# A Poisson loss kernel: loads of two rows per partition, three buffers per input, and a tapered last group

## The chip, the cores and the metric

The kernel runs on one core of one Trainium2 chip. The metric is device time in microseconds (us); a profile taken of one of the executions adds the span from its first to its last instruction, which is some 2 us shorter. All runs reported here are of the fast state, with a granted clock of 1.0. "Unit" below means 128 columns, 512 bytes in each partition. SBUF and PSUM are the two on-chip memories in which the kernels place their tiles, here 128 partitions each. "The same", "faster" and "slower" are meant by a rule of 2%, with a 95% interval for the ratio.

## The reference

```python
# log_input, target: float32 [1024, 4096]
def reference(log_input, target):
    loss = np.exp(log_input) - target * log_input
    return np.mean(loss, axis=-1).astype(np.float32)
```

Two inputs of 16.8 MB each are read once, 1024 numbers are written. ScalarE (ACT) does the exp with its row sum, VectorE (DVE) the product with its row sum.

## The kernel before

Partition p holds rows 8p to 8p+7, so a load of one "row block" takes one row of 16 KB for each of 128 partitions. Four buffers per input; the last row block is cut into pieces of 2048, 1024, 512 and 512 columns.

```python
x_blk = log_input.rearrange("(p b) d -> b p d", b=nb)      # nb = 8
last_bounds = [0, 2048, 3072, 3584, 4096]
io_pool = ctx.enter_context(tc.tile_pool(name="io", bufs=4))
for b in range(nb):
    # ... bounds = [0, d], or last_bounds for the last block
    for c in range(ncy):
        # ... x_tile, t_tile from io_pool
        nc.sync.dma_start(out=x_tile[:, :w], in_=x_blk[b, :, lo:hi])
        nc.sync.dma_start(out=t_tile[:, :w], in_=t_blk[b, :, lo:hi])
        # ACT: exp of x into a bf16 scratch in SBUF, row sum into exp_sums
        # DVE: -t * x into a bf16 scratch, row sum into prod_sums
    # DVE: comb = sum(exp_sums + prod_sums) / d  -> all_loss[:, b]
nc.sync.dma_start(out=out_blk, in_=all_loss)
```

Of the kernel before, what the change touches and what calls it, by code (L numbers as in the profile page):

```python
# [2 lines left out]

# [4 lines left out]


@with_exitstack
def kernel(
    ctx: ExitStack,
    tc: tile.TileContext,
    log_input: bass.AP,
    target: bass.AP,
    out: bass.AP,
):
    nc = tc.nc
    P = nc.NUM_PARTITIONS  # L20
    fp32 = mybir.dt.float32
    bf16 = mybir.dt.bfloat16

    n, d = log_input.shape
    assert target.shape == (n, d)
    assert out.shape == (n,)

    nb = (n + P - 1) // P
    assert nb * P == n, "row count must be a multiple of 128"
    inv_d = 1.0 / d  # L30

    x_blk = log_input.rearrange("(p b) d -> b p d", b=nb)
    t_blk = target.rearrange("(p b) d -> b p d", b=nb)
    out_blk = out.rearrange("(p b) -> p b", b=nb)

    full_bounds = [0, d]
    if d == 4096:
        last_bounds = [0, 2048, 3072, 3584, 4096]
    else:
        last_bounds = [0]  # L40
        rem = d
        while rem > max(512, d // 8):
            rem //= 2
            last_bounds.append(d - rem)
        last_bounds.append(d)
        last_bounds = sorted(set(last_bounds))
    max_chunks = max(len(full_bounds), len(last_bounds)) - 1

    io_pool = ctx.enter_context(tc.tile_pool(name="io", bufs=4))
    accum_pool = ctx.enter_context(tc.tile_pool(name="accum", bufs=4))  # L50
    out_pool = ctx.enter_context(tc.tile_pool(name="outp", bufs=1))
    scratch_pool = ctx.enter_context(tc.tile_pool(name="scratch", bufs=2))

    all_loss = out_pool.tile([P, nb], fp32)

    for b in range(nb):
        bounds = last_bounds if b == nb - 1 else full_bounds
        ncy = len(bounds) - 1

        exp_sums = accum_pool.tile([P, max_chunks], fp32, name="exp_sums")  # L60
        prod_sums = accum_pool.tile([P, max_chunks], fp32, name="prod_sums")

        for c in range(ncy):
            lo, hi = bounds[c], bounds[c + 1]
            w = hi - lo
            x_tile = io_pool.tile([P, d], fp32, name="x_tile")
            t_tile = io_pool.tile([P, d], fp32, name="t_tile")
            nc.sync.dma_start(out=x_tile[:, :w], in_=x_blk[b, :, lo:hi])  # L68
            nc.sync.dma_start(out=t_tile[:, :w], in_=t_blk[b, :, lo:hi])  # L69

            e_scr = scratch_pool.tile([P, d], bf16, name="e_scr")
            nc.scalar.activation(  # L72
                out=e_scr[:, :w],
                in_=x_tile[:, :w],
                func=mybir.ActivationFunctionType.Exp,
                bias=0.0,
                scale=1.0,
                accum_out=exp_sums[:, c:c + 1],
            )

            p_scr = scratch_pool.tile([P, d], bf16, name="p_scr")
            nc.vector.tensor_tensor_reduce(  # L82
                out=p_scr[:, :w],
                in0=t_tile[:, :w],
                in1=x_tile[:, :w],
                scale=-1.0,
                scalar=0.0,
                op0=mybir.AluOpType.mult,
                op1=mybir.AluOpType.add,
                accum_out=prod_sums[:, c:c + 1],  # L90
            )

        comb = accum_pool.tile([P, max_chunks], fp32, name="comb")
        nc.vector.tensor_tensor_reduce(  # L94
            out=comb[:, :ncy],
            in0=exp_sums[:, :ncy],
            in1=prod_sums[:, :ncy],
            scale=inv_d,
            scalar=0.0,
            op0=mybir.AluOpType.add,  # L100
            op1=mybir.AluOpType.add,
            accum_out=all_loss[:, b:b + 1],
        )

    nc.sync.dma_start(out=out_blk, in_=all_loss)


# [1 line left out]
_INS = ['log_input', 'target']  # L109
_OUTS = [((1024,), 'float32')]  # L110


# [23 lines left out]
```

## Time and profile before

| | before |
|---|---|
| device time, median | 87.24 us (87.16 to 87.39, 3 runs) |
| span of the profile | 85.2 us |
| bytes read | 33.55 MB, 394 GB/s over the span |
| first data packet / last load landed / store issued | 1.73 / 81.67 / 82.88 us |

The page's groups of instructions say where the engines wait (columns: line, engine, operation, tiles, shapes and count; then busy us and mean ns of one; then the idle time ahead of the group and what ended it):

```profile
L82 DVE CUSTOM_DVE_ANT_0 p_scr<-t_tile,x_tile 128x4096 bf16<-128x4096 f32 (+3 forms) x11 | 35.9, 3261 | 44.4 <-DMA t_tile<-in_target_dram 44.2
L72 ACT ACTIVATE e_scr<-x_tile 128x4096 bf16<-128x4096 f32 (+3 forms) x11 | 29.5, 2685 | 49.3 <-DMA x_tile<-in_log_input_dram 43.2
```

DVE works 36 us and waits 44 us for t; ACT works 30 us and waits for x. Both wait for the stream.

Beside its views, the trace holds a record of each DMA packet (start, duration, bytes) on the 16 DMA engines, and the text uses those: one packet is one contiguous run of one partition, one descriptor (the 14 loads of 16 KB rows are 1792 packets of 16,384 bytes, 128 each). That makes 8 packets per engine for a load of one row block, and after them each engine makes a 4-byte completion write (352 for 22 loads). "Last completions" below is the mean over the 16 engines of the start of their last completion write of the loads, counted from the first data packet.

### The profile page before, as it was taken

To read this page: it belongs to the slowest core of one execution; us is meant where nothing else is said; L and a number is where in the kernel's file an instruction comes from. 1 tells how busy PE (TensorE), PEld (TensorE's weight loads), DVE (VectorE), ACT (ScalarE), POOL (GpSimd) and SP (SyncE) were. 2 spreads that over 40 slices of the span, in tenths; PEclk is the share of its full clock that TensorE was granted. 3 is DMA by queue.
4 is the path that set the end of the run, shared out by engine and by line. 5 is a ranking of instruction groups with operands and counts; after the bars stand their busy time and mean duration, and the time that the engine had idled before them with its cause. 6 is when DMAs were issued, how large, how long until landed. Compare 5 with 4: busy or idle time off the path is not lost.

```text
span 85.2 us, 165 instructions
## 1 busy us (share of the span) xinstructions
DVE 37.3 (44%) x38; ACT 31.8 (37%) x23; POOL 0.2 (0%) x4
## 2 busy tenths in 40 slices
DVE  0000009920398007930199005950099103989750
ACT  6002940079000960049200880029400690274430
POOL 0000000000000000000000000000000000000000
DMA  5699999999999999999998989899999999999900
GB/s 123 277 462 400 462 400 462 400 462 400 462 400 462 400 462 400 462 400 462 385 477 369 492 369 485 377 462 400 454 408 431 431 431 396 419 406 401 387 22 2
DMA packets 3312, 33.56 MB, mean 394 GB/s; under 512 B 496, under 2 KB 496, under 8 KB 1264
## 3 DMA queue, kind: packets, MB, share of 16 engines
q1 hardware_dynamic: 3312, 33.56, 93.9%
HBM read 33.55 MB, written 0.00 MB: 394 GB/s over the span
## 4 chain that ended last, share of the span: by engine, by line
DMA 80%; DVE 11%; SPq 3%; issue 1%; DVEq 0%
DMA t_tile<-in_target_dram 80%; DVE p_scr L82 11%; SPq L68 2%; SPq L69 1%; DVE comb L94 0%; DVEq L82 0%; DVE prod_sums L82 0%; DVEq L94 0%; DVEq L131 0%
## 5 line engine op out<-in xcount | busy, mean ns | idle before, releaser
L82 DVE CUSTOM_DVE_ANT_0 p_scr<-t_tile,x_tile 128x4096 bf16<-128x4096 f32 (+3 forms) x11 | 35.9, 3261 | 44.4 <-DMA t_tile<-in_target_dram 44.2
L72 ACT ACTIVATE e_scr<-x_tile 128x4096 bf16<-128x4096 f32 (+3 forms) x11 | 29.5, 2685 | 49.3 <-DMA x_tile<-in_log_input_dram 43.2
L72 ACT ACTIVATION_READ_ACCUMULATOR e_scr<-x_tile 128x1 f32 x11 | 2.0, 186 | 0.0
L94 DVE CUSTOM_DVE_ANT_0 comb<-exp_sums,prod_sums 128x1 f32<-128x1 f32 (+1 forms) x8 | 1.3, 160 | 1.2
L72 ACT ACT_TABLE_LOAD x1 | 1.3, 1283 | 0.7 <-PEq L120 0.7
L82 DVE DVE_READ_ACCUMULATOR2_ANT prod_sums<- 128x1 f32 x11 | 0.9, 82 | 0.0
L94 DVE DVE_READ_ACCUMULATOR2_ANT all_loss<- 128x1 f32 x8 | 0.7, 82 | 0.0
L120 POOL MEMSET const-uint8-127<- 128x1 uint8 x1 | 0.1, 102 | 0.0
L120 POOL MEMSET const-bfloat16-1.0<- 128x1 bf16 x1 | 0.1, 101 | 0.0
L120 POOL MEMSET const-float32-0.0<- 128x1 f32 x1 | 0.1, 98 | 0.2 <-issue 0.2
L120 POOL MEMSET const-float32-1.0<- 128x1 f32 x1 | 0.1, 98 | 0.0
## 6 DMA issues: line engine op xcount, KB each, us to landing
x_tile<-in_log_input_dram SPq DMA_DIRECT2D x7, 2048.0 KB, 29.6
t_tile<-in_target_dram SPq DMA_DIRECT2D x7, 2048.0 KB, 34.1
x_tile<-in_log_input_dram SPq DMA_DIRECT2D x1, 1024.0 KB, 27.2
t_tile<-in_target_dram SPq DMA_DIRECT2D x1, 1024.0 KB, 29.3
x_tile<-in_log_input_dram SPq DMA_DIRECT2D x1, 512.0 KB, 21.2
t_tile<-in_target_dram SPq DMA_DIRECT2D x1, 512.0 KB, 22.1
x_tile<-in_log_input_dram SPq DMA_DIRECT2D x2, 256.0 KB, 9.2
t_tile<-in_target_dram SPq DMA_DIRECT2D x2, 256.0 KB, 9.5
```

The costliest lines, as they stand in the source:

```text
L68: nc.sync.dma_start(out=x_tile[:, :w], in_=x_blk[b, :, lo:hi])
L69: nc.sync.dma_start(out=t_tile[:, :w], in_=t_blk[b, :, lo:hi])
L72: nc.scalar.activation(out=e_scr[:, :w], in_=x_tile[:, :w], func=mybir.ActivationFunctionType.Exp, bias=0.0, scale=1.0, accum_out=exp_sums ...
L82: nc.vector.tensor_tensor_reduce(out=p_scr[:, :w], in0=t_tile[:, :w], in1=x_tile[:, :w], scale=-1.0, scalar=0.0, op0=mybir.AluOpType.mult, ...
L94: nc.vector.tensor_tensor_reduce(out=comb[:, :ncy], in0=exp_sums[:, :ncy], in1=prod_sums[:, :ncy], scale=inv_d, scalar=0.0, op0=mybir.AluO ...
L120: nc = _bacc.Bacc("TRN2", target_bir_lowering=False, num_devices=1)
```

## The change

Its intent: move the same bytes in longer runs and fewer transfers, hold more of them in SBUF, and leave less work behind the last byte. Rows are taken in pairs (32 KB runs); the exp's unused output goes to PSUM and the product over t, in place of scratch tiles in SBUF (four of 8 KB per partition), and each input has three 32 KB buffers; the last group is cut so that x comes ahead of t, and the last product takes all earlier sums as a pointer scalar (one start value per partition, read from SBUF, in place of a constant), so that no combine, the small instruction that adds up a row's sums, follows it.

```diff
-    io_pool = ctx.enter_context(tc.tile_pool(name="io", bufs=4))
+    x_v = log_input.rearrange("(p g r) d -> g p (r d)", g=groups, r=2)
+    tail = [
+        ("x", 32 * u), ("t", 32 * u), ("x", 24 * u), ("t", 12 * u), ("t", 12 * u),
+        ("x", 6 * u), ("t", 5 * u), ("x", 2 * u), ("t", 3 * u),
+    ]
+    io = ctx.enter_context(tc.tile_pool(name="io", bufs=3))
+    dump = ctx.enter_context(tc.tile_pool(name="dump", bufs=1, space=bass.MemoryType.PSUM))
 ...
+    for g in range(groups - 1):
+        x_tile = io.tile([P, 2 * d], F32, name="x_tile")
+        t_tile = io.tile([P, 2 * d], F32, name="t_tile")
+        nc.sync.dma_start(out=x_tile, in_=x_v[g])
+        nc.sync.dma_start(out=t_tile, in_=t_v[g])
 ...  # for each of the two rows: exp_sum, prod_sum (over t), combine
+    for what, w in tail:
 ...
+                combine(slice(nb - 1, k["t"]), so_far)
+                prod_sum(x_tile, t_tile, s, -inv_d, so_far, all_loss[:, b : b + 1])
```

More of the change, by code (lines that the diff above doesn't have):

```diff
@@ L2 @@
-import math
 from contextlib import ExitStack
@@ L8 @@
 from concourse._compat import with_exitstack
+ACT_F = mybir.ActivationFunctionType
+ALU = mybir.AluOpType
+F32 = mybir.dt.float32
 @with_exitstack
@@ L20 @@
     P = nc.NUM_PARTITIONS
-    fp32 = mybir.dt.float32
-    bf16 = mybir.dt.bfloat16
     n, d = log_input.shape
-    assert target.shape == (n, d)
-    assert out.shape == (n,)
-    nb = (n + P - 1) // P
-    assert nb * P == n, "row count must be a multiple of 128"
+    nb = n // P
+    assert nb * P == n and tuple(target.shape) == (n, d) and nb % 2 == 0
+    assert d % 32 == 0
     inv_d = 1.0 / d
-    x_blk = log_input.rearrange("(p b) d -> b p d", b=nb)
-    t_blk = target.rearrange("(p b) d -> b p d", b=nb)
@@ L34 @@
-    out_blk = out.rearrange("(p b) -> p b", b=nb)
-    full_bounds = [0, d]
-    if d == 4096:
-        last_bounds = [0, 2048, 3072, 3584, 4096]
-    else:
-        last_bounds = [0]
-        rem = d
-        while rem > max(512, d // 8):
-            rem //= 2
-            last_bounds.append(d - rem)
-        last_bounds.append(d)
-        last_bounds = sorted(set(last_bounds))
-    max_chunks = max(len(full_bounds), len(last_bounds)) - 1
-    io_pool = ctx.enter_context(tc.tile_pool(name="io", bufs=4))
@@ L50 @@
-    accum_pool = ctx.enter_context(tc.tile_pool(name="accum", bufs=4))
-    out_pool = ctx.enter_context(tc.tile_pool(name="outp", bufs=1))
-    scratch_pool = ctx.enter_context(tc.tile_pool(name="scratch", bufs=2))
-    all_loss = out_pool.tile([P, nb], fp32)
-    for b in range(nb):
-        bounds = last_bounds if b == nb - 1 else full_bounds
-        ncy = len(bounds) - 1
-        exp_sums = accum_pool.tile([P, max_chunks], fp32, name="exp_sums")
-        prod_sums = accum_pool.tile([P, max_chunks], fp32, name="prod_sums")
-        for c in range(ncy):
-            lo, hi = bounds[c], bounds[c + 1]
-            w = hi - lo
-            x_tile = io_pool.tile([P, d], fp32, name="x_tile")
-            t_tile = io_pool.tile([P, d], fp32, name="t_tile")
-            nc.sync.dma_start(out=x_tile[:, :w], in_=x_blk[b, :, lo:hi])
-            nc.sync.dma_start(out=t_tile[:, :w], in_=t_blk[b, :, lo:hi])
-            e_scr = scratch_pool.tile([P, d], bf16, name="e_scr")
-            nc.scalar.activation(
-                out=e_scr[:, :w],
-                in_=x_tile[:, :w],
-                func=mybir.ActivationFunctionType.Exp,
-                bias=0.0,
-                scale=1.0,
-                accum_out=exp_sums[:, c:c + 1],
-            )
-            p_scr = scratch_pool.tile([P, d], bf16, name="p_scr")
-            nc.vector.tensor_tensor_reduce(
-                out=p_scr[:, :w],
-                in0=t_tile[:, :w],
-                in1=x_tile[:, :w],
-                scale=-1.0,
-                scalar=0.0,
-                op0=mybir.AluOpType.mult,
-                op1=mybir.AluOpType.add,
-                accum_out=prod_sums[:, c:c + 1],
-            )
-        comb = accum_pool.tile([P, max_chunks], fp32, name="comb")
-        nc.vector.tensor_tensor_reduce(
-            out=comb[:, :ncy],
-            in0=exp_sums[:, :ncy],
-            in1=prod_sums[:, :ncy],
@@ new lines @@
+    groups = nb // 2
+    u = d // 32
+    x_v = log_input.rearrange("(p g r) d -> g p (r d)", g=groups, r=2)
+    t_v = target.rearrange("(p g r) d -> g p (r d)", g=groups, r=2)
+    out_v = out.rearrange("(p b) -> p b", b=nb)
+    tail = [
[3 more added lines that the diff above has]
+    io = ctx.enter_context(tc.tile_pool(name="io", bufs=3))
+    small = ctx.enter_context(tc.tile_pool(name="small", bufs=1))
@@ new lines, with exp_sum @@
+    dump = ctx.enter_context(tc.tile_pool(name="dump", bufs=1, space=bass.MemoryType.PSUM))
+    exp_sums = small.tile([P, nb + 4], F32, name="exp_sums")
+    prod_sums = small.tile([P, nb + 4], F32, name="prod_sums")
+    comb = small.tile([P, nb], F32, name="comb")
+    so_far = small.tile([P, 1], F32, name="so_far")
+    all_loss = small.tile([P, nb], F32, name="all_loss")
+    def exp_sum(x_tile, s, k):
+        e_scr = dump.tile([P, d], F32, name="e_scr")
+        nc.scalar.activation(
+            out=e_scr[:, : s.stop - s.start],
+            in_=x_tile[:, s],
+            func=ACT_F.Exp,
+            bias=0.0,
+            scale=1.0,
+            accum_out=exp_sums[:, k : k + 1],
+        )
@@ new lines, in prod_sum, with combine @@
+    def prod_sum(x_tile, t_tile, s, scale, start, accum):
+        nc.vector.tensor_tensor_reduce(
+            out=t_tile[:, s],
+            in0=t_tile[:, s],
+            in1=x_tile[:, s],
+            scale=scale,
+            scalar=start,
+            op0=ALU.mult,
+            op1=ALU.add,
+            accum_out=accum,
+        )
+    def combine(k, accum):
+        nc.vector.tensor_tensor_reduce(
+            out=comb[:, : k.stop - k.start],
+            in0=exp_sums[:, k],
+            in1=prod_sums[:, k],
@@ L98 @@
             scale=inv_d,
             scalar=0.0,
-            op0=mybir.AluOpType.add,
-            op1=mybir.AluOpType.add,
-            accum_out=all_loss[:, b:b + 1],
-        )
-    nc.sync.dma_start(out=out_blk, in_=all_loss)
+            op0=ALU.add,
+            op1=ALU.add,
+            accum_out=accum,
+        )
+    for g in range(groups - 1):
[3 more added lines that the diff above has]
+        nc.sync.dma_start(out=t_tile, in_=t_v[g])
+        for r in range(2):
+            b = 2 * g + r
+            s = slice(r * d, (r + 1) * d)
+            exp_sum(x_tile, s, b)
+            prod_sum(x_tile, t_tile, s, -1.0, 0.0, prod_sums[:, b : b + 1])
+            combine(slice(b, b + 1), all_loss[:, b : b + 1])
@@ new lines @@
+    g, b = groups - 1, nb - 1
+    x_tile = io.tile([P, 2 * d], F32, name="x_tile")
+    t_tile = io.tile([P, 2 * d], F32, name="t_tile")
+    at = {"x": 0, "t": 0}
+    k = {"x": nb - 2, "t": nb - 2}
+    for what, w in tail:
+        s = slice(at[what], at[what] + w)
+        at[what] += w
+        if what == "x":
+            nc.sync.dma_start(out=x_tile[:, s], in_=x_v[g, :, s])
+            exp_sum(x_tile, s, k["x"])
+        else:
+            nc.sync.dma_start(out=t_tile[:, s], in_=t_v[g, :, s])
+            if s.stop < 2 * d:
+                prod_sum(x_tile, t_tile, s, -1.0, 0.0, prod_sums[:, k["t"] : k["t"] + 1])
+                if s.stop == d:
+                    combine(slice(nb - 2, nb - 1), all_loss[:, b - 1 : b])
+            else:
+                combine(slice(nb - 1, k["t"]), so_far)
+                prod_sum(x_tile, t_tile, s, -inv_d, so_far, all_loss[:, b : b + 1])
+        k[what] += 1
@@ L109 @@
+    assert at == {"x": 2 * d, "t": 2 * d} and k["x"] == k["t"] - 1 == nb + 2
+    nc.sync.dma_start(out=out_v, in_=all_loss)
 _INS = ['log_input', 'target']
```

## The prediction

> **What bounds the kernel now.** I read the page first: engines, slices, queue, chain. The question it answers is which resource is full from start to end.
>
> ```profile
> DVE 37.3 (44%) x38; ACT 31.8 (37%) x23; POOL 0.2 (0%) x4
> DMA  5699999999999999999998989899999999999900
> DMA packets 3312, 33.56 MB, mean 394 GB/s; under 512 B 496, under 2 KB 496, under 8 KB 1264
> q1 hardware_dynamic: 3312, 33.56, 93.9%
> DMA 80%; DVE 11%; SPq 3%; issue 1%; DVEq 0%
> ```
>
> Neither compute engine is half busy. The DMA row is at 9 from the third slice until the loads are in, and the chain is 80% one kind of wait, a landing of the target tensor. So the kernel is a stream of 33.55 MB with a start before it and a tail behind it, and a change can win only in three places: the rate of the stream, its start, and what follows its last byte.
>
> The stretches of time give the rate (columns: stretch, its length, busy us of DVE, ACT and POOL, clock, DMA share, GB/s):
>
> ```profile
> 12.00:22.00 10.00, 4.60 (x4) 3.71 (x2) 0.00 (x0) 1.00 1.01 434
> 22.00:71.00 49.00, 23.01 (x20) 18.55 (x10) 0.00 (x0) 1.00 1.00 428
> 71.00:76.00 5.00, 4.41 (x2) 1.96 (x2) 0.00 (x0) 1.00 1.00 415
> 76.00:79.00 3.00, 2.49 (x6) 1.20 (x3) 0.00 (x0) 1.00 1.02 402
> 79.00:81.00 2.00, 1.71 (x3) 0.72 (x2) 0.00 (x0) 1.00 1.04 381
> ```
>
> The share stays at 1.00 or above in all five, so the queue never ran dry; yet the rate falls from 428 to 381 GB/s as the pieces of the last row block get smaller. That is a cost for each descriptor. The packet records of the trace give it directly. Median times on an engine: 612 ns for 16 KB, 312 for 8 KB, 162 for 4 KB, 87 for 2 KB, 9 for a 4-byte completion write. The first four lie on one line: 12 ns plus 36.6 ns per KB (16,384 bytes in 600 ns; 16 engines: 437 GB/s).
>
> Last the chain in order of time (start, us, what), for what follows the last landing:
>
> ```profile
> 76.46 5.21 DMA t_tile<-in_target_dram
> 81.67 0.03 issue
> 81.70 0.05 DVEq L82
> 81.75 0.08 issue
> 81.84 0.69 DVE p_scr L82
> 82.53 0.02 DVE prod_sums L82
> ...
> 82.68 0.16 DVE comb L94
> ```
>
> From the landing at 81.67 there are 0.17 us to the start of the last product, 0.69 for it, 0.15 to the combine and 0.16 for that; the store is issued at 82.88, 1.21 us after the landing. The remaining 2.3 us of the span are the store and the end of the program, which the change leaves alone.
>
> [...]
>
> **The change part by part.**
>
> *Rows of 32 KB.* Before, each of 16 engines handles 8 partitions of each load: 14 loads of 16 KB make 112 descriptors, and the eight tail pieces 64 more (16 of 8 KB, 16 of 4 KB, 32 of 2 KB): 176. After, six loads of 32 KB make 48, and nine pieces of the last group 72: 120. The 56 fewer descriptors are worth 56 x 12 = 0.67 us. Loads fall from 22 to 15, so 7 completion writes of 9 ns go: 0.06. Together 0.73 us, all of it on the path, because the engines are never idle. A check of this model on the kernel before: 2,097,152 bytes per engine at 600 ns per 16,384 are 76.8 us, 176 x 12 are 2.1, 22 x 9 are 0.2: 79.1 us. The packet records run from 1.7 to 81.2 us, 79.4, and the first packets took up to 1420 ns instead of 612; that accounts for the rest.
>
> *Three buffers per input.* The last group's loads wait for the first group's buffers. I put the first t landing at about 22 us and its two products at 2 x 4.43 us, so the buffers are free near 31.5. Five more 4 MB loads are then queued or in flight, enough until about 61 us. The builder's order of instructions also shows that each load waits for the completion of the eighth load before it, as its eight completion semaphores come round; with these sizes each such landing is over ten microseconds ahead of need. So no hole: worth 0.
>
> *In-place product, exp into PSUM.* The product writes fp32 over t instead of bf16 elsewhere[...]. Both engines have over 50% idle time in the stream. Worth 0 there.
>
> *The tail.* The last t piece is 384 wide instead of 512[...], and no combine stands behind it; but now a combine (so_far) stands ahead of it, and that needs the exp of the last x piece. I set the last landing to T. A piece of n units (512 bytes per partition) takes 8 x (18.75n + 12) + 9 ns, so the landings are: x of 2 units T-0.56, t of 5 T-0.96, x of 6 T-1.82, second t of 12 T-2.82, first T-4.73. ACT, by 0.203 us plus 0.833 ns per element (fitted to 512: 630 and 4096: 3616): the 768 exp runs from T-1.65 and is out with its accumulator read by T-0.71; the 256 exp starts at T-0.39, takes 0.42, with the read it ends at T+0.12. DVE: the 1536 products (1.76 us each) end at T-2.80 and T-0.89, the 640 one runs from T-0.79 to T+0.04. The combine can start near T+0.2, so_far is there at T+0.38, the last product starts after 0.15 more at T+0.54 and ends at T+1.10, the store goes out at T+1.13. Before it was T+1.21. Gain 0.08, well within the error of these gaps.
>
> *Start.* The first load is issued and its first packet starts as before. Worth 0.
>
> Sum: 0.73 + 0.08 = 0.81 us; 87.24 - 0.81 = 86.43. I round it to 86.45.
>
> **The rivals.**
>
> *The 32 KB rows are cut again.* [...]the count is 168 instead of 120, and the gain is 8 x 12 + 63 = 0.16 us for the stream: about 87.0. Nothing in the trace before has a row over 16 KB, so it speaks neither way; I give it one chance in five.
>
> *A new wait in the tail.* The new order chains exp, accumulator read, combine and product after the last x landing, and puts the 640 product ahead of it. If each hand-over between engines costs 0.1 us more than I took, or a product with a pointer scalar starts later, the store goes out at T+1.4: a loss of 0.2 instead of a gain of 0.08, 86.7. For it speaks that the margin between DVE and ACT is under 0.2 us; against it that each link has a measured duration.
>
> *A hole in the stream.* If the last group's issue were held longer than I think, DMA would idle between groups and the time would rise by some microseconds. Against it: about 30 us of margin. I give it 2%.
>
> *A large gain.* It would need the start or the rate to move. The start is latency ahead of the first packet; with no descriptor cost at all the rate would gain 2.1 us, 2.4%, and the change keeps over two thirds of the descriptors. I give it 2%.
>
> **Range and chances.** The middle is 86.45; the split rows or the longer tail lie to 87.0, both together near 87.25. On the lower side, a shorter tail (PSUM as destination, a smaller gap ahead of the last product) gives at most 0.3. The runs of before spread over 0.23 us. So 86.05 to 87.0 in 8 of 10. Faster by over 2% would be under 85.5: 0.02. Slower by over 2% would be above 89.0: 0.02. The rest, 0.96, is within 2%.
>
> **What would show each step right or wrong.** The queue's packet count: 48 x 16 + 72 x 16 data packets, 128 of the store and 16 x 16 completions are 2304; 3072 would mean split rows. A 32 KB packet of about 1212 ns. First exp near 12.5 us, first product near 22.3, later first products of a group 19.4 us apart (two loads of 8 x 1.212 + 0.009), not 19.57 (twice the 9.785 us between products now). DMA row at 9 until the last landing, which comes near 80.9 instead of 81.67. Store issued about 1.1 us after it. The prediction is wrong if any slice in the middle falls below 9, if the landing stays at 81.5 or later without split rows, or if the store follows the last landing by more than 1.5 us.

The sum came to 0.81 us, 0.73 for the stream and 0.08 for the tail; the working for the last product had 0.56 us for 384 columns, where 512 took 0.69. The tail's product times are estimates, and the trace before gives the same ones: the line through its products of 512 and 4096 columns (692 and 4425 ns) comes to 1.76 us for 1536 columns, 0.83 for 640 and 0.56 for 384; measured later were 1758 and 826 ns, and 559 for 384 in e3. That a product over t takes as long as before was not shown then; for 4096 columns it took 4423 ns against 4425. Cut rows mean 168 packets per engine, two of 16 KB for each 32 KB row; why they should be cut was not shown. The wait for the eighth load before is in the changed kernel's trace: its loads 12 to 15 were issued at 41.90, 51.61, 61.33 and 66.22 us, 0.02 us after loads 4 to 7 had landed. The "at most 0.3" for a shorter tail is the author's estimate without working; what PSUM gave is 29 ns per exp (e6).

## The result, and the profile after

The changed kernel takes 86.69 us (86.65 to 86.79, 4 runs) against 87.31 for the kernel before in the same job (87.16 to 87.40): ratio 0.9934, 95% interval 0.9920 to 0.9948. A ratio here is the mean time of one kernel's fast runs over the mean of the other's fast runs of the same rounds, so it is not quite the ratio of the medians quoted. By the 2% rule this is "same"; the gain of 0.62 us is small but clear of noise. A repeat in another job gave 0.9966.

The page of the changed kernel, the same rows as in the prediction:

```profile
DVE 36.8 (44%) x38; ACT 31.5 (37%) x21; POOL 0.2 (0%) x4
DMA  8597999799979997999799979997999999999900
DMA packets 2304, 33.56 MB, mean 397 GB/s; under 512 B 384, under 2 KB 640, under 8 KB 1152
q1 hardware_dynamic: 2304, 33.56, 93.7%
DMA 92%; SPq 2%; DVE 2%; issue 1%; DVEq 0%
```

The packets are 2304, exactly the count for whole 32 KB rows. The time of all packets is 93.7% of 84.6 us, 79.3 us per engine, against 93.9% of 85.2, 80.0 us: it fell by 0.7 us, about the predicted amount. The stream itself did not end 0.7 us earlier, but about 0.5. DVE's share of the chain fell from 11% to 2% because the chain no longer passes through a product that frees a buffer: it is one run of landings.

The 7s in the DMA row are not idle engines. The view counts a packet whole in the slice in which it starts, which is why slices of 496 GB/s stand beside slices of 325. The 16 engines run nearly in step (their completions of one load lie within 0.42 us) with 1.2 us packets, and slices are 2.1 us long; in a run below with 8 KB packets the same row is 9 all through, with a later end. The completions of the changed kernel's 4 MB loads come 9.681 to 9.712 us apart with no gap.

The stretches of time:

```profile
22.00:71.00 49.00, 27.09 (x24) 18.54 (x10) 0.00 (x0) 1.00 0.99 426
71.00:76.00 5.00, 4.60 (x4) 1.11 (x1) 0.00 (x0) 1.00 0.99 415
76.00:79.00 3.00, 2.15 (x3) 1.74 (x2) 0.00 (x0) 1.00 0.99 400
```

The share is 0.99 where it was 1.00 to 1.02 before, at much the same rate. These last digits alone would prove little, as a packet counts where it starts. The records show what is behind them: in the kernel before, eight packets of 2 KB and a completion write last 8 x 87 + 9 = 705 ns, but the completions of such loads come 676 to 680 ns apart. So the packets of one engine overlap a little in time, here by 4%, while for the 32 KB packets (8 x 1213 + 9 = 9713 ns, steps of up to 9712) the overlap is all but gone.

The end of the chain in order of time, and the row of DMA issues for the last piece:

```profile
80.54 0.83 DVE t_tile L70
81.37 0.02 DVE prod_sums L70
...
81.52 0.14 DVE comb L82
81.65 0.05 DVE so_far L82
81.70 0.04 issue
81.74 0.62 DVE t_tile L70
```

```profile
t_tile<-in_target_dram SPq DMA_DIRECT2D x1, 192.0 KB, 15.0
```

The last t piece was issued at 66.22 us and took 15.0 to land, so the last landing T is at 81.2 (81.23 in the record of landings), 0.44 earlier than before (81.67). The store goes out at 82.39, T+1.16, against T+1.21 before. The last product does not wait for that landing, but for the product and the combine ahead of it.

| | before | after |
|---|---|---|
| packets of data per engine | 176 | 120 |
| last completions (mean of engines) | 79.34 | 78.82 |
| last landing | 81.67 | 81.23 |
| store issued | 82.88 | 82.39 |
| span | 85.2 | 84.6 |

### The profile page after: what moved, and what is told of

Its sections match the earlier page's. It is cut to its first block, busy times and chain, and to the rows that moved or that the text cites. A ratio compares the mean times of both kernels' runs of the same rounds, so it can differ in the third digit from the quotient of the medians.

```text
span 84.6 us, 144 instructions
## 1 busy us (share of the span) xinstructions
DVE 36.8 (44%) x38; ACT 31.5 (37%) x21; POOL 0.2 (0%) x4
## 2 busy tenths in 40 slices
DMA packets 2304, 33.56 MB, mean 397 GB/s; under 512 B 384, under 2 KB 640, under 8 KB 1152
## 3 DMA queue, kind: packets, MB, share of 16 engines
q1 hardware_dynamic: 2304, 33.56, 93.7%
## 4 chain that ended last, share of the span: by engine, by line
DMA 92%; SPq 2%; DVE 2%; issue 1%; DVEq 0%
DMA x_tile<-in_log_input_dram 58%; DMA t_tile<-in_target_dram 34%; DVE t_tile L70 2%; SPq L97 1%; SPq L96 1%; DVE comb L82 0%; DVE so_far L82 0%; DVEq L82 0%; DVEq L70 0%; DVE prod_sums L70 0%; DVEq L154 0%
## 5 line engine op out<-in xcount | busy, mean ns | idle before, releaser
L70 DVE CUSTOM_DVE_ANT_0 t_tile<-t_tile,x_tile 128x4096 f32<-128x4096 f32 (+2 forms) x10 | 35.1, 3530 | 44.7 <-DMA t_tile<-in_target_dram 44.7
L60 ACT ACTIVATE e_scr<-x_tile 128x4096 f32<-128x4096 f32 (+3 forms) x10 | 29.0, 2905 | 49.1 <-DMA x_tile<-in_log_input_dram 49.0
L70 DVE CUSTOM_DVE_ANT_0 t_tile<-t_tile,x_tile,so_far 128x384 f32<-128x384 f32 x1 | 0.6, 619 | 0.1
```

The costliest lines, as they stand in the source:

```text
L60: nc.scalar.activation(out=e_scr[:, : s.stop - s.start], in_=x_tile[:, s], func=ACT_F.Exp, bias=0.0, scale=1.0, accum_out=exp_sums[:, k : ...
L70: nc.vector.tensor_tensor_reduce(out=t_tile[:, s], in0=t_tile[:, s], in1=x_tile[:, s], scale=scale, scalar=start, op0=ALU.mult, op1=ALU.ad ...
```

## The experiments

The main theory: the gain is the 56 descriptors that went, at about 8 ns of elapsed time each, not the 12 ns that the packet durations suggested. Rivals: buffers, scratch or the tail made the gain.

### Rows of 16 KB in the changed kernel (e1)

```diff
-        nc.sync.dma_start(out=x_tile, in_=x_v[g])
-        nc.sync.dma_start(out=t_tile, in_=t_v[g])
+        for r in range(2):
+            h = slice(r * d, (r + 1) * d)
+            nc.sync.dma_start(out=x_tile[:, h], in_=x_v[g, :, h])
+            nc.sync.dma_start(out=t_tile[:, h], in_=t_v[g, :, h])
```

> The changed kernel with its six 32 KB-row loads cut back to twelve of 16 KB rows, all else kept: 48 more descriptors on each DMA engine and 6 more completion writes of 9 ns. Theory A (the gain is descriptors, each worth about 8 ns of elapsed time, as the steps between completions suggest): 48 x 8 + 6 x 9 = 0.44 us more than the changed kernel, about 87.1 us. Theory B (12 ns each, as my prediction had it): 0.63 us more, about 87.3. Rival C (the gain comes from buffers, scratch or the tail, and row length is worth nothing): no change, 86.7.

86.99 us median (86.94 to 88.05) against 87.20 for the kernel before; ratio 0.9997 (0.9963 to 1.0030), widened by the one run at 88.05. By the medians two thirds of the gain are gone (0.21 us left of 0.62). Last completions: 79.28, 0.47 later than the changed kernel's 78.82. Taking off six completions of 9 ns, 48 descriptors cost 0.41 us: 8.6 ns each. By these completions rival C falls, and 8 ns fits better than 12; the times alone would not settle it, as the interval of this ratio takes in the 0.9966 of the changed kernel's repeat (e9 below).

### The kernel before with 32 KB rows (e2)

```diff
-    io_pool = ctx.enter_context(tc.tile_pool(name="io", bufs=4))
+    io_pool = ctx.enter_context(tc.tile_pool(name="io", bufs=2))
-    scratch_pool = ctx.enter_context(tc.tile_pool(name="scratch", bufs=2))
+    scratch_pool = ctx.enter_context(tc.tile_pool(name="scratch", bufs=1))
 ...
-            x_tile = io_pool.tile([P, d], fp32, name="x_tile")
-            t_tile = io_pool.tile([P, d], fp32, name="t_tile")
-            nc.sync.dma_start(out=x_tile[:, :w], in_=x_blk[b, :, lo:hi])
-            nc.sync.dma_start(out=t_tile[:, :w], in_=t_blk[b, :, lo:hi])
+            if b < nb - 2:
+                if b % 2 == 0:
+                    # ... x_pair, t_pair [P, 2 * d]
+                    nc.sync.dma_start(out=x_pair, in_=x2_blk[b // 2])
+                    nc.sync.dma_start(out=t_pair, in_=t2_blk[b // 2])
+                # ... the half of the pair that holds row b
+            else:
+                # ... rows 6 and 7 in pieces as before, one tile for all pieces of a row
-                out=p_scr[:, :w],
+                out=t_tile[:, :w],
```

> The kernel before with only its first six row blocks loaded as three pairs of 32 KB rows, its tail and its combines kept (the product is written over t to make room). 48 descriptors and 6 completion writes fewer than before. Theory A (8 ns): 0.44 us faster than before, about 86.87. Theory B (12 ns): 0.63 faster, about 86.7. Rival C (row length worth nothing): as before, 87.3.

86.64 us median (86.56 to 87.19) against 87.20; ratio 0.9945 (0.9926 to 0.9963), which is 0.32 to 0.65 us. The interval holds A and just holds B; the packet records speak for A: last completions at 78.96, 0.37 earlier than in the kernel before, or 6.7 ns for each of 48 descriptors. So the long rows give nearly the whole gain in the old kernel, without the PSUM destination, the new pieces and the fold. (Buffers and scratch were changed with them here; e7 shows that two buffers are no gain of their own.)

### The combine after the last product (e3)

```diff
+    nc.vector.memset(exp_sums, 0.0)
-                combine(slice(nb - 1, k["t"]), so_far)
-                prod_sum(x_tile, t_tile, s, -inv_d, so_far, all_loss[:, b : b + 1])
+                prod_sum(x_tile, t_tile, s, -1.0, 0.0, prod_sums[:, k["t"] : k["t"] + 1])
+                combine(slice(nb - 1, k["t"] + 1), all_loss[:, b : b + 1])
```

> The changed kernel with the last product not folded: no pointer scalar, a combine of four columns after it instead of one of three ahead of it. The last product can then start as soon as the product ahead of it is done, about 0.2 us after the last landing instead of 0.51, takes 0.56 instead of 0.62, and 0.32 us of gap and combine follow: store at about T+1.1, against T+1.16 now. Theory: within 0.1 us of the changed kernel (86.6 to 86.7). Rival (the fold is where the tail gains): slower by 0.3 us, 87.0.

86.50 us median (86.35 to 86.62) against 87.20; ratio 0.9921 (0.9908 to 0.9934). Its last completions are the changed kernel's (78.83), and its end in the chain reads:

```profile
81.36 0.56 DVE t_tile L72
81.92 0.02 DVE prod_sums L72
...
82.07 0.17 DVE comb L84
```

The store goes out at 82.27 instead of 82.39, with the last landing at 81.23 in both. In these profiles the fold of the combine into the last product is thus no gain but a loss of about 0.1 us: the combine and the 0.15 us ahead of it stand on DVE either way, the fold adds a second hand-over (0.04 us, from the combine to the product), and the product with a pointer scalar takes 619 ns where the one without takes 559. (The memset clears a column that the combine reads and no exp fills.)

### The old pieces in the changed kernel (e4)

```diff
-        ("x", 32 * u), ("t", 32 * u), ("x", 24 * u), ("t", 12 * u), ("t", 12 * u),
-        ("x", 6 * u), ("t", 5 * u), ("x", 2 * u), ("t", 3 * u),
+        ("x", 32 * u), ("t", 32 * u), ("x", 16 * u), ("t", 16 * u), ("x", 8 * u), ("t", 8 * u),
+        ("x", 4 * u), ("t", 4 * u), ("x", 4 * u), ("t", 4 * u),
```

(The combine stands last here too, as in e3.)

> The changed kernel with the pieces of the kernel before in its last row block (2048, 1024, 512, 512 for each input, x and t by turns, combine last). Eight descriptors and one completion write more (0.07 us by 8 ns) and the store at T+1.21 instead of T+1.16: 0.12 us more than the changed kernel, about 86.8. Rival (the taper is most of the gain): 0.4 to 0.6 more, 87.1 to 87.3.

86.74 us median (86.54 to 87.06) against 87.20; ratio 0.9949 (0.9935 to 0.9963), by that 0.1 us behind the changed kernel. Last completions 78.94. As expected, for the pieces and the fold together. What the pieces alone are worth is seen against e3, which has the same order of combine and ran in the same job; the two stores, e3 and then this run:

```profile
82.27 0.35 SPq L130 DMA_DIRECT2D out_dram<-all_loss  x1
82.48 0.35 SPq L131 DMA_DIRECT2D out_dram<-all_loss  x1
```

The old pieces are 0.21 us later (0.24 by the ratios 0.9949 and 0.9921). So the taper is worth about 0.2 us, half of it in earlier completions (78.83 against 78.94), and the fold took about half of that back.

### A dose of descriptors (e5)

```diff
-        nc.sync.dma_start(out=x_tile, in_=x_v[g])
+        for h in (slice(0, d // 2), slice(d // 2, d)):
+            nc.sync.dma_start(
+                out=x_tile.rearrange("p (r d) -> p r d", r=2)[:, :, h],
+                in_=x_v[g].rearrange("p (r d) -> p r d", r=2)[:, :, h],
+            )
 ...  # t likewise
```

> A dose: the changed kernel with each 4 MB load made as two of half the columns of both rows, so that every run is 8 KB: 192 descriptors of 8 KB per engine in place of 48 of 32 KB, 144 more, and 6 more completion writes. Theory A (8 ns elapsed per descriptor): 144 x 8 + 54 = 1.2 us more than the changed kernel, about 87.9. Theory B (12 ns): 1.8 us more, about 88.5. If row length is worth nothing: 86.7.

88.00 us median (87.90 to 88.11) against 87.31; ratio 1.0072 (1.0050 to 1.0094). Relative to the kernel before it lost 0.69 us by the medians where the changed kernel gained 0.62: 1.3 us apart, and A said 1.2, B 1.8. Last completions 80.22, 1.40 later for 144 descriptors and six completions: 9.4 ns each. This run and e1 have the same 21 loads and differ in 96 descriptors alone; their completions lie 0.93 us apart, 9.7 ns each, so it is not the number of loads that costs. Its page:

```profile
DMA  3899999999999999999999999999999999999900
DMA packets 4704, 33.56 MB, mean 390 GB/s; under 512 B 480, under 2 KB 736, under 8 KB 1248
```

The engines look busier than in the changed kernel, and the kernel is slower.

### Exp to SBUF again (e6)

```diff
-    dump = ctx.enter_context(tc.tile_pool(name="dump", bufs=1, space=bass.MemoryType.PSUM))
+    dump = ctx.enter_context(tc.tile_pool(name="dump", bufs=1))
-        e_scr = dump.tile([P, d], F32, name="e_scr")
+        e_scr = dump.tile([P, d], mybir.dt.bfloat16, name="e_scr")
```

> The changed kernel with the exp written as bf16 to SBUF again instead of fp32 to PSUM. My theory (both engines idle over half the time, the 256-wide exp is not what the combine waits for last): no change within 0.1 us, exp of 4096 back at about 3.62 us. Rival (less traffic on SBUF is part of the stream's gain): 0.1 to 0.3 us slower and later completions in the packet records.

86.60 us median (86.40 to 86.89) against 87.31; ratio 0.9914 (0.9888 to 0.9941). Exp of 4096 took 3616 ns again, against 3587 with PSUM; last completions 78.88 against 78.82. An fp32 result in PSUM in place of a bf16 one in SBUF (place and type changed together) gives the engine 29 ns per exp (388 ns against 417 for 256 columns too) and the kernel nothing.

### Two buffers (e7)

```diff
-    io = ctx.enter_context(tc.tile_pool(name="io", bufs=3))
+    io = ctx.enter_context(tc.tile_pool(name="io", bufs=2))
```

> The changed kernel with two buffers per input instead of three. The third group's loads then wait for the first group's products, free near 31.5 us, while the queue holds loads until about 41 us. Theory: no hole, no change within 0.1 us (86.7). Rival (three buffers are needed to keep the queue full): a hole of microseconds, 88 or more, and a slice of the DMA row well below 9.

86.59 us median (86.37 to 86.86) against 87.31; ratio 0.9915 (0.9889 to 0.9940), last completions 78.84. The third group's loads waited 28.7 us for a product, and the stream did not notice:

```profile
SPq L96 <- DVE prod_sums L70: 28.7, 1, 28.7
```

The third buffer is worth nothing. (This run's DMA row has single slices of 6 and 7, as the changed kernel's has 7s, so that part of the expectation was badly chosen; the completions are 9.681 to 9.718 us apart.)

### Rows of 48 KB (e8): a miss

```diff
-    io = ctx.enter_context(tc.tile_pool(name="io", bufs=3))
+    io = ctx.enter_context(tc.tile_pool(name="io", bufs=2))
-    for g in range(groups - 1):
-        x_tile = io.tile([P, 2 * d], F32, name="x_tile")
+    for g in range(2):
+        x_tile = io.tile([P, 3 * d], F32, name="x_tile")
 ...  # t likewise
+        nc.sync.dma_start(out=x_tile[:, : 3 * d], in_=x_r[:, 3 * g * d : 3 * (g + 1) * d])
-        for r in range(2):
+        for r in range(3):
```

> The change carried one step further: groups of three, three and two rows, so four loads of 48 KB rows in place of six of 32 KB: 16 descriptors and 2 completion writes fewer, two buffers per input. Theory A (8 ns): 16 x 8 + 18 = 0.15 us faster than the changed kernel, about 86.55. Theory B (12 ns): 0.21 faster, 86.5. The packet records should show 512 packets of 49152 bytes of about 1815 ns; if rows over 32 KB are cut, no gain. First buffers free near 45 us with loads queued to 60, so no hole.

88.96 us median (88.90 to 89.36) against 87.31; ratio 1.0188 (1.0162 to 1.0213), by the 2% rule unclear. Expected was 0.15 us faster than the changed kernel; it is more than 2 us slower. The stream is not to blame: 512 packets of 49,152 bytes of 1815 ns, last completions 78.74, the earliest of all. DVE in order of time (start, us, engine, line, what) shows where the time went:

```profile
61.38 4.43 DVE L73 CUSTOM_DVE_ANT_0 t_tile<-t_tile,x_tile 128x4096 f32<-128x4096 f32 x1 [15.46 <-DMA t_tile<-in_target_dram]
...
70.15 4.42 DVE L73 CUSTOM_DVE_ANT_0 t_tile<-t_tile,x_tile 128x4096 f32<-128x4096 f32 x1
...
74.58 4.42 DVE L73 CUSTOM_DVE_ANT_0 t_tile<-t_tile,x_tile 128x4096 f32<-128x4096 f32 x1
...
79.42 1.76 DVE L73 CUSTOM_DVE_ANT_0 t_tile<-t_tile,x_tile 128x1536 f32<-128x1536 f32 x1
```

After a wait of 15.46 us three rows of t land at once near 61 us, and from there DVE works back to back: three products, then row 6 (in the changed kernel that product starts at 71.23, here at 74.58), then the pieces. The store goes out at 84.63. DVE is idle over half the span (busy 42% of it), and still the bound at the end. I had asked only whether the queue runs dry.

### The 48 KB rows at the start (e11)

```diff
-    io = ctx.enter_context(tc.tile_pool(name="io", bufs=3))
+    io = ctx.enter_context(tc.tile_pool(name="io", bufs=1))
-    for g in range(groups - 1):
-        x_tile = io.tile([P, 2 * d], F32, name="x_tile")
+    for g, (b0, nr) in enumerate([(0, 3), (3, 2), (5, 1)]):
+        x_tile = io.tile([P, nr * d], F32, name="x_tile" + str(nr))
 ...  # t likewise; the last two rows in pieces as in the changed kernel, in the first group's tiles
```

> Groups of 3, 2 and 1 rows, then the last two as in the changed kernel: as many loads and descriptors as the changed kernel, with the 48 KB rows at the start and small groups late. Theory D (the run with 48 KB rows lost its time because three products of 4.43 us still stood on VectorE when the last rows came in, not because 48 KB rows are slow): no loss, within 0.1 us of the changed kernel. Rival E (48 KB rows or the deeper buffer are slow in themselves): over a microsecond slower.

87.00 us median (86.78 to 87.03) against 87.30; ratio 0.9964 (0.9952 to 0.9976), and the changed kernel in the same job 0.9966. Theory D holds: 48 KB rows cost nothing where DVE has time to work them off, and give nothing with as many descriptors.

### The changed kernel again (e9)

No edit.

> The changed kernel itself, word for word, so that the runs beside it are compared on one chip. It should repeat 0.993 of the kernel before, 86.6 to 86.75 us.

86.86 us median (86.74 to 87.34) against 87.30; ratio 0.9966 (0.9946 to 0.9985). The median is just outside the range I gave. Two of six runs (87.34, 87.17) stand apart from the other four (86.74 to 86.87). So a difference of 0.2 us between jobs says nothing, and e6 and e7 at 0.991 can't be called faster than the changed kernel; nor can e3 by its time alone.

### A shorter tail (e10, and again as e12)

```diff
-        ("x", 32 * u), ("t", 32 * u), ("x", 24 * u), ("t", 12 * u), ("t", 12 * u),
-        ("x", 6 * u), ("t", 5 * u), ("x", 2 * u), ("t", 3 * u),
+        ("x", 32 * u), ("t", 32 * u), ("x", 18 * u), ("t", 17 * u),
+        ("x", 8 * u), ("t", 9 * u), ("x", 4 * u), ("t", 4 * u), ("x", 2 * u), ("t", 2 * u),
```

(with the combine last, as in e3)

> A candidate to beat both kernels: the changed kernel with the combine after the last product (as in the run with the combine last) and the last row in halving pieces, x ahead of t each time: x 18, t 17, x 8, t 9, x 4, t 4, x 2, t 2 units of 128 columns. One piece more (8 descriptors and a completion, 0.07 us), but the last product is 256 wide (0.43 us) and not behind a combine: store at about T+0.95 instead of T+1.16. Theory: 0.1 us faster than the changed kernel. Rival (the tail is at its floor, the extra piece costs what the shorter end gives): no difference.

86.55 us median (86.31 to 87.03) against 87.30; ratio 0.9914 (0.9897 to 0.9931), where the changed kernel in the same job had 0.9966 (0.9946 to 0.9985).

> The candidate with the halving tail and the combine last once more, in another job, because the changed kernel moved by 0.003 of the ratio between two jobs. If the candidate's lead is real, its ratio to the kernel before stays at or below 0.992; if it was chance, it comes out between 0.993 and 0.997 like the changed kernel. If its profiled execution isn't a delayed one this time, the store is issued near 82.3 us, against 82.4 in the changed kernel.

86.39 us median (86.35 to 87.25) against 87.25; ratio 0.9901 (0.9884 to 0.9917). The lead is real, though under 2%: at the medians this version beats the changed kernel by 0.3 us in the same job, and the kernel before by 0.75 and 0.86 us. The time between the slowest engine's last completion write and the store is 1.36 us in e10's profile and 1.34 in e12's, against 1.63 in the changed kernel and 1.68 in the one before, so most of the lead is the end. In e3 that time is 1.50, so the combine last and the new pieces have about half each; by the whole time e3 (0.9921 in another job) was not compared with this version.

The runs of this version fall in two sets, though: 86.35 to 86.39 in four of six of e12, 87.11 and 87.25 in the others. Both profiled executions (87.03 and 87.25) were delayed ones, so the 82.3 us store of a quick one was never seen. In both, packets of the first uneven x piece (9,216 bytes) took up to 669 and 600 ns instead of 347, and the engines' last completions spread over 0.7 and 1.0 us instead of 0.3 to 0.5. But this is not where the mean fell behind: the eighth load, the last ahead of that piece, is complete at 68.98 and 69.15 us (mean of the engines, counted as before) where e4, with the same count of packets and loads, has 68.73, and the last completions, 79.24 and 79.40, are later than e4's 78.94 by much the same. The delay came in the even 16 and 32 KB loads ahead (after the start a 32 KB packet took up to 1331 and 1332 ns for 1213). The changed kernel's second profile (e9) has slow packets in its first uneven piece too (12,288 bytes, up to 633 ns for 460) and ends as early as others (78.87); its first profile has none. What delays packets was not tried and stays open.

## Why the prediction was right

The measured 86.69 us lies in the predicted range (86.05 to 87.0), and "within 2%" was right. The repeat, 86.86, lies in it too. The predicted gain was 0.8 us, the measured one 0.62 in that job and 0.44 by the medians of the repeat. Point by point:

**What bounds it: right.** In every run the store followed the stream, except e8, where DVE's backlog did.

**The descriptor count: right.** 120 per engine, 2304 packets in all, no row cut; a 32 KB packet took 1213 ns, 1212 predicted. The rival of cut rows falls.

**The cost of a descriptor: mis-sized.** This is the step that failed: "The 56 fewer descriptors are worth 56 x 12 = 0.67 us". The 12 ns came from a line through packet durations, and packets of one engine overlap (705 ns of durations in a step of 676 to 680 for loads of 2 KB packets), so durations count some time twice. The steps between completions count it once. (The "36.6 ns per KB" of the prediction is per 1000 bytes.) A 2 MB load of 16 KB rows steps by 4.893 us in mid-stream: less 9 ns, by 8, 610.5 ns per packet. The slow 32 KB step, 9.712, gives 1212.9 in the same way. The second 16 KB costs 602.4 of these, so a descriptor costs 8.1 ns. Then 56 x 8 + 7 x 9 ns is 0.51 us, and the last completions moved by 0.52 in the mean of the engines (0.44 for the slowest engine). The prediction held two hints of this. Its own forecast of 19.4 us per group after 19.57 before, from the steps between products, is worth about 9 ns per descriptor, not 12. And its check of the model (79.1 of 79.4 us) closed only because it left 0.3 us for the start: the first load of the kernel before is complete 5.63 us after the first data packet, 0.77 more than the 4.862 us of the steps that follow it. Over the experiments:

| kernel | packets per engine | loads | last completions, us |
|---|---|---|---|
| before | 176 | 22 | 79.34 |
| e1, 16 KB rows | 168 | 21 | 79.28 |
| e2, before with 32 KB rows | 128 | 16 | 78.96 |
| e4, old pieces | 128 | 16 | 78.94 |
| changed; e9, the same again; e11 | 120 | 15 | 78.82; 78.87; 78.96 |
| e8, 48 KB rows | 104 | 13 | 78.74 |
| e5, 8 KB runs | 264 | 21 | 80.22 |

The kernels with 120 packets, e3, e6 and e7 among them (78.83, 78.88, 78.84), differ by up to 0.14, so e8's step is within scatter; e5 against the changed kernel is ten times it. "Cost of a descriptor" stands here for whatever comes with one more run of the same bytes: no run changes the number of descriptors and keeps the length of the runs, so the two are not told apart. The figure isn't constant either: the first five loads of the kernel before step by 4.862, which by the same working is about 4 ns. Why it is lower there no run tells. My own fences held a third hint: a DMA share of 1.02 and 1.04 for small pieces, which I read only as "never ran dry".

**Three buffers worth 0: right**, shown by e7. **PSUM and the product in place worth 0: right** for PSUM (e6); the product in place was not undone alone, but e2 carries it, its product of 4096 takes 4423 ns against 4425, and it shows no loss.

**The tail: right in sum, partly by luck.** Store at T+1.13 predicted, T+1.16 found. The 640 product ended at T+0.14 instead of T+0.04, but the last product followed so_far after 0.04 us instead of 0.15, and so started at T+0.51, close to the T+0.54 of the prediction, by two errors that cancel. It took 619 ns instead of 0.56 us. This chain was the second rival, and it took about 0.04 us of the 0.08.

**The checks that I named.** First exp 12.78 (12.5) and first product 22.60 (22.3), both 0.3 late, and the prediction does not show how it came to these two; the first products of groups 0 and 2 at 22.60 and 61.45, so 19.4 us per group (19.4). Last landing 81.2 (80.9), of which 0.2 is the descriptor error again. "The prediction is wrong if any slice in the middle falls below 9" was a bad test: long packets alone make the row uneven, and the row before has three 8s itself, which the prediction read as a row of 9s.

## What to carry to other kernels

Where a stream is the bound, take the cost of a descriptor from the time between completions (8.1 ns here), not from packet durations (12 ns), and multiply it by the count first: 56 fewer were worth half a microsecond of 87. Size a load also by what it leaves for the engines when it lands: a group that lands late with more work than the time left makes an engine with half its time idle the bound (e8). Folding the last combine into an instruction that must wait for it was not a saving here (e3); cutting the last row so that less is left at its end was (e4 against e3, e10).
